# A feed-forward down projection with seven-product operands: the order of the products, the place of three kinds of stores and the pace of the operand fetches

## The chip, the cores and the metric

The kernel runs on one core of one Trainium2 chip. The time is that of the whole kernel on the device, in microseconds; of the kernel before, three runs are given. The core has a matrix engine (TensorE, PE in the profile), VectorE (DVE), ScalarE (ACT), GpSimd (POOL) and SyncE (SP), which here does nothing but issue DMAs, one after the other in the order of its queue.

## The reference

The reference is one layer of a hybrid transformer on 640 tokens (512 of a latent grid, 128 of a prompt): latent attention and a two-way RWKV-7 scan side by side, an output projection, and a SwiGLU feed-forward with post-normalisation. The change lies in the feed-forward, whose part is:

```python
def _swiglu(h, p):
    return (jax.nn.silu(h @ p["w_ffn_gate"]) * (h @ p["w_ffn_up"])) @ p["w_ffn_down"]
...
    x = _post_norm(x, g2, _swiglu(x * (1 + sc2) + sh2, p), p["ln2_g"], p["ln2_b"])
```

The model width is 2048, the hidden width 5632.

## The kernel before

**Seven products.** Gate, up and down projection are multiplied by a Strassen-like scheme. Two neighbouring 128-wide rows of the output and the two halves of the tokens (320 each) form a 2x2 block, and seven products of sums of blocks take the place of eight. Each product is written as three matmuls in a rounded format (high x high, high x low, low x high), 128x128 against 128x320.

**The right-hand operands.** For each pair of hidden tiles there are seven tiles of 128x640, numbered 0 to 6: tile 0 serves product 1, tiles 1 and 2 serve products 5 and 7, tiles 3 and 4 serve 4 and 6, tiles 5 and 6 serve 2 and 3. For the down projection they are made by `stored` (L1699), one step after each product of the next gate pair, with casts on ScalarE, differences on VectorE and subtractions on GpSimd, and go to DRAM (`hd`). There are 22 pairs of hidden tiles. The last pair has no gate pair behind it: its steps are kept as the generator `last` and run in the down projection's very first output pair (L1824).

**The weights.** `Quads.units` (L1372) loads four blocks 0 to 3 for each pair of output rows (`raw`, ten buffers, `N_R`), forms the seven sums in the order of the products, and splits each into high and low (`qh`, `ql`, four buffers, `N_Q`): a granule. A pair of the gate or up projection or of the down projection's pieces 1 to 3 has two granules for each product, one of piece 0 has one. Three granules are made ahead of the one that TensorE works on. Product 7 takes block 0 minus block 2 (GpSimd), product 5 the sum of 2 and 3, product 6 that less block 0 (both VectorE), product 4 block 3, product 2 block 1, product 3 block 1 less what stands in block 0 (GpSimd). Each block of the next pair is loaded where the same block of this pair is done with (`ahead`).

**The order of the products** is `ORDER` (L1329), for all three projections; `strassen` (L1437) walks through it, sends each product's result on with `out`, and calls `next(beside)` after each product.

**The down projection** runs over four pieces `c` of the hidden width, with 4, 6, 6 and 6 hidden pairs (`sizes`), and in each over eight pairs `j` of output rows. A piece needs 28 or 42 operand tiles in SBUF. The sums are carried in DRAM between the pieces: for each pair two `z` tiles are loaded (`sums_ahead`, L1804) and, a pair later, stored (`sums_behind`, L1811). Piece 3 makes products 1, 7, 5, 6, 3 of every pair first, and 2 and 4 at the end, beside the last normalisation.

**What sets the order.** SP's queue is in program order from the last up pair to the second pair of piece 3; everywhere else, and on the other engines, a scheduler with its own time line sets it. `Fetch` (L1722) fetches the operand tiles of the next piece: `step`, called at each granule, issues one as long as `room` allows; `room` is set at `j == 1` to `N_F - 7 * npr - 7` (28 in piece 0, 14 in pieces 1 and 2) and grows in the last pair as products let go of their tiles (`released`, L1750). What is missing when a product is written down is fetched there, by `operand` (L1743). SP waits, for each DMA, for the eighth DMA before it to land.

Of the kernel before, what the change touches and what calls it, by code (L numbers as in the profile page):

```python
# [157 lines left out]
def step_kernel(ctx: ExitStack, tc: tile.TileContext, a: dict, o: dict, upto: int = 99, npairs: int = NPAIR, dbg=None):  # L158
# [1169 lines left out]

    ORDER = (1, 7, 5, 6, 2, 3, 4)  # L1329

    class Quads:
# [40 lines left out]
        def units(self, pairs, begun=0, later=0):  # L1372
# [3 lines left out]
            for n, src in enumerate(pairs):  # L1376
                ng = src.shape[1]
                gs = range(ng)
                whole = n < len(pairs) - later
                q = nxt or {}  # L1380
# [6 lines left out]
                def ahead(k):  # L1387
                    if n + 1 < len(pairs):
                        for g in range(pairs[n + 1].shape[1]):
                            nxt[k, g] = self.load(pairs[n + 1][k, g])  # L1390
# [15 lines left out]
                ahead(2)  # L1406
                for g in gs:
                    if n >= begun and whole:
                        yield self.split(q[1, g])
                    tt(G, q[1, g], q[1, g], q.pop((0, g)), ALU.subtract)  # L1410
# [3 lines left out]
                ahead(1)  # L1414
                for g in gs if whole else ():
                    yield self.split(q.pop((3, g)))
                ahead(3)

# [303 lines left out]
    class Fetch:  # L1722
# [3 lines left out]
        def __init__(self, k0, n):  # L1726
            self.k0, self.t, self.room, self.count = k0, [[None] * 7 for _ in range(n)], 0, 0
            self.order = [(i, m) for q in ((0,), (1, 2), (3, 4), (5, 6)) for i in range(n) for m in q]

# [9 lines left out]
        def step(self):  # L1739
            if self.count < min(self.room, len(self.order)):  # L1740
                self.fetch()
# [8 lines left out]
        def released(self, n):  # L1750


            for m in ORDER:
                self.room += n * {1: 1, 5: 2, 3: 2, 4: 2}.get(m, 0)
                yield
# [15 lines left out]
    fetch = Fetch(0, 4)  # L1771
# [44 lines left out]
    def moved(c, j, n):  # L1816

        rel = fetch.released(n) if fetch and j == 7 else None
        for k in range(len(ORDER)):
            if k == 1:  # L1820
                sums_behind()
            if k == 2 and (c, j) != (3, 7):
                sums_ahead(*((c, j + 1) if j < 7 else (c + 1, 0)))
            if c + j == 0:  # L1824
                next(last, None)
            if rel:
                next(rel)
            yield

    sums_ahead(0, 0)  # L1830
    for c, (npr, ng) in enumerate(sizes):
        ops, k0 = fetch, k0 + npr
        fetch = qs.beside = Fetch(k0, sizes[c + 1][0]) if c < 3 else None
        for j in range(8):
            if j == 1 and fetch:
                fetch.room = N_F - 7 * npr - 7
# [170 lines left out]
```

## Time and profile before

| | us |
|---|---|
| median of 3 runs (lowest, highest) | 3575.87 (3572.85, 3577.72) |
| profiled execution: time, span | 3577.47, 3575.7 |
| TensorE busy in the span | 3391.9 (95%) |
| VectorE busy | 2627.2 (73%) |
| ScalarE busy | 1460.2 (41%) |
| GpSimd busy | 994.1 (28%) |
| first matmul of the down projection, from the span's start | 2916.33 |
| mean granted clock of TensorE | 0.959 |

All times in the views count from the start of the span. A row of a timeline shows when an instruction started, how long it took, its engine, line, operation and tiles, and in brackets how long the engine stood idle before it and what ended the wait. Buffer numbers are left out of the names: `op` is an operand tile, `hd` its place in DRAM, `raw` a block of weights, `b` a bank of PSUM, `z` a tile of sums and `zd` its place in DRAM, `p` and `t` the operand tiles that are made in SBUF.

### The profile page before, as it was taken

What the parts mean: (1) busy time and instruction counts of PE and PEld (TensorE: products, weight loads), DVE (VectorE), ACT (ScalarE), POOL (GpSimd) and SP (SyncE); (2) the same over time, 40 slices, a digit from 0 to 9 for tenths busy, and PEclk for the clock granted to TensorE, in tenths of its full rate; (3) what the DMA queues carried; (4) which work ended last, traced back from release to release, by engine and by line L of the source; (5) the groups of instructions that cost most, each with busy time, mean ns of one, the idle gap of its engine ahead of it and who ended that gap; (6) DMA issues with size and microseconds to landing.
All of it is one profiled execution on the core that took longest, in us unless ns stands there. A gap on an engine that the chain in (4) does not pass through costs nothing. (4 is left out here: it accounts for less than half of the span.)

```text
span 3575.7 us, 71303 instructions
## 1 busy us (share of the span) xinstructions
PE 3391.9 (95%) x27538; PEld 3032.9 (85%) x27538; DVE 2627.2 (73%) x4721; ACT 1460.2 (41%) x2987; POOL 994.1 (28%) x944
## 2 busy tenths in 40 slices
PE   8979999999999999999979999999999989999987
PEld 4667776777887778889979999999999989999987
DVE  1355676666676776667788988888888868778898
ACT  1143333333444444444453444444444434334334
POOL 0021111111111212111164544444444432222245
PEclk9988999999998999999989999999999999999997
DMA  8653444444112111066534443444433468666743
GB/s 296 236 171 125 142 152 138 155 153 137 60 58 86 37 41 37 18 215 196 154 113 136 165 129 128 133 138 138 136 124 127 143 227 296 234 245 213 257 126 106
DMA packets 289716, 529.05 MB, mean 148 GB/s; under 512 B 31008, under 2 KB 83680, under 8 KB 289376
## 3 DMA queue, kind: packets, MB, share of 16 engines
q1 hardware_dynamic: 289376, 524.49, 44.6%
q8 instruction: 216, 3.54, 0.4%
q14 instruction: 124, 1.02, 0.1%
HBM read 429.65 MB, written 93.09 MB: 146 GB/s over the span
## 5 line engine op out<-in xcount | busy, mean ns | idle before, releaser
L226 DVE TENSOR_TENSOR ql<-raw,qh 128x512 fp32r<-128x512 f32 (+1 forms) x1136 | 932.2, 834 | 282.9 <-ACT qh L1290 270.4
L1290 ACT CAST qh<-raw 128x512 fp32r<-128x512 f32 (+1 forms) x1136 | 661.0, 589 | 880.5 <-PE b L112 658.2
L226 POOL TENSOR_TENSOR raw<-raw,raw 128x512 f32<-128x512 f32 (+1 forms) x288 | 405.6, 1412 | 824.0 <-DVE ql L226 577.7
L112 PE MATMUL b<-t,qh 128*128 128x320 f32 x2816 | 626.9, 310 | 7.9 <-ACT qh L1290 6.8
L112 PE MATMUL b<-op,qh 128*128 128x320 f32 x2464 | 555.0, 318 | 26.0 <-DMA op<-hd 12.7
L112 PEld LDWEIGHTS b<-t,qh 128*128 128x128 f32 x2816 | 473.7, 189 | 9.1 <-ACT qh L1290 7.5
L112 PE MATMUL b<-p,qh 128*128 128x320 f32 x2112 | 468.2, 310 | 0.7 <-ACT qh L1290 0.7
L112 PEld LDWEIGHTS b<-op,qh 128*128 128x128 f32 x2464 | 422.2, 194 | 37.0 <-DMA op<-hd 15.7
L112 PE MATMUL b<-t,ql 128*128 128x320 f32 x1408 | 436.9, 311 | 5.8 <-DVE ql L226 5.8
L112 PE MATMUL b<-op,ql 128*128 128x320 f32 x1232 | 378.0, 319 | 17.0 <-DVE ql L226 17.0
L112 PEld LDWEIGHTS b<-p,qh 128*128 128x128 f32 x2112 | 354.3, 188 | 1.3 <-ACT qh L1290 1.2
L112 PE MATMUL b<-p,ql 128*128 128x320 f32 x1056 | 327.9, 311 | 7.0 <-DVE ql L226 7.0
L112 PEld LDWEIGHTS b<-t,ql 128*128 128x128 f32 x1408 | 265.2, 188 | 8.7 <-DVE ql L226 8.6
L112 PEld LDWEIGHTS b<-op,ql 128*128 128x128 f32 x1232 | 235.2, 194 | 25.4 <-DVE ql L226 25.0
L226 DVE TENSOR_TENSOR raw<-raw,raw 128x512 f32<-128x512 f32 (+1 forms) x288 | 246.4, 866 | 11.5 <-POOL raw L226 5.8
L112 PE MATMUL acc<-xh,whi 128*128 128x320 f32 x928 | 239.7, 341 | 0.3 <-DVE vS L1145 0.2
L112 PE MATMUL acc<-xh,wlo 128*128 128x320 f32 x928 | 235.6, 336 | 0.8 <-DVE wlo L226 0.8
L112 PE MATMUL b<-mh,qh 128*128 128x320 f32 x1024 | 229.6, 313 | 7.0 <-ACT qh L1290 7.0
L112 PE MATMUL acc<-xl,whi 128*128 128x320 f32 x928 | 236.2, 337 | 0.0
L112 PEld LDWEIGHTS b<-p,ql 128*128 128x128 f32 x1056 | 198.9, 188 | 9.4 <-DVE ql L226 9.4
L263 ACT CAST whi<-raw 128x512 fp32r<-128x512 f32 (+1 forms) x156 | 95.0, 609 | 257.1 <-PE acc L112 167.4
L226 DVE TENSOR_TENSOR wlo<-raw,whi 128x512 fp32r<-128x512 f32 (+1 forms) x156 | 107.3, 688 | 111.4 <-ACT whi L263 79.5
(328 smaller groups left out, 5847.5 us busy)
## 6 DMA issues: line engine op xcount, KB each, us to landing
wm<-in_w_mod_dram SPq DMA_DIRECT2D x64, 1024.0 KB, 5.4
op<-hd SPq DMA_DIRECT2D x154, 320.0 KB, 6.0
raw<-in_w_gate_dram SPq DMA_DIRECT2D x188, 256.0 KB, 2.7
raw<-in_w_up_dram SPq DMA_DIRECT2D x188, 256.0 KB, 2.8
raw<-in_w_down_dram SPq DMA_DIRECT2D x224, 192.0 KB, 3.5
raw<-in_w_in_dram SPq DMA_DIRECT2D x132, 256.0 KB, 2.7
wm<-in_w_mod_dram SPq DMA_DIRECT2D x64, 512.0 KB, 6.2
raw<-in_w_out_dram SPq DMA_DIRECT2D x128, 256.0 KB, 3.2
```

The costliest lines, as they stand in the source:

```text
L112: self.eng.matmul(out, lhsT, rhs, start=start, stop=stop)
L226: eng.tensor_tensor(out=out, in0=x, in1=y, op=op)
L263: A.copy(hi, r)
L1290: A.copy(hi, x)
```

## The change

The products come in the order 1, 7, 5, 6, 4, 2, 3, so block 3 of the weights is split ahead of block 1, and its successor is loaded ahead of those of blocks 0 and 1; the tiles 3 and 4 are let go ahead of 5 and 6. The stores of sums move from after the second product to after the fifth (`k == 4`), their loads from after the third to after the fourth (`k == 3`). The steps of `last` move from the first output pair of piece 0 to the third. `Fetch.step` issues at every second call until `released` starts, and in piece 0 the room for it opens at `j == 3` instead of `j == 1`.

```diff
@@ -1326,7 +1326,7 @@
                 out[t - 2] = third(*out[t - 2])
         return out
 
-    ORDER = (1, 7, 5, 6, 2, 3, 4)
+    ORDER = (1, 7, 5, 6, 4, 2, 3)
 
     class Quads:
 
@@ -1405,6 +1405,11 @@
                     yield self.split(q[0, g])
                 ahead(2)
                 for g in gs:
+                    if whole:
+                        yield self.split(q[3, g])
+                    del q[3, g]
+                ahead(3)
+                for g in gs:
                     if n >= begun and whole:
                         yield self.split(q[1, g])
                     tt(G, q[1, g], q[1, g], q.pop((0, g)), ALU.subtract)
@@ -1412,9 +1417,6 @@
                 for g in gs:
                     yield self.split(q.pop((1, g)))
                 ahead(1)
-                for g in gs if whole else ():
-                    yield self.split(q.pop((3, g)))
-                ahead(3)
 
     def product(qs, ops, ng, m):
         npr = len(ops) // ng
@@ -1725,6 +1727,7 @@
 
         def __init__(self, k0, n):
             self.k0, self.t, self.room, self.count = k0, [[None] * 7 for _ in range(n)], 0, 0
+            self.every, self.turn = 2, 0
             self.order = [(i, m) for q in ((0,), (1, 2), (3, 4), (5, 6)) for i in range(n) for m in q]
 
         def __len__(self):
@@ -1737,7 +1740,8 @@
             DMA.dma_start(out=t.bitcast(F32), in_=h_d[self.k0 + i][m])
 
         def step(self):
-            if self.count < min(self.room, len(self.order)):
+            self.turn += 1
+            if self.turn % self.every == 0 and self.count < min(self.room, len(self.order)):
                 self.fetch()
 
         def operand(self, i, m):
@@ -1750,8 +1754,9 @@
         def released(self, n):
 
 
+            self.every = 1
             for m in ORDER:
-                self.room += n * {1: 1, 5: 2, 3: 2, 4: 2}.get(m, 0)
+                self.room += n * {1: 1, 5: 2, 4: 2, 3: 2}.get(m, 0)
                 yield
 
     begun, beside = [], None
@@ -1817,11 +1822,11 @@
 
         rel = fetch.released(n) if fetch and j == 7 else None
         for k in range(len(ORDER)):
-            if k == 1:
+            if k == 4:
                 sums_behind()
-            if k == 2 and (c, j) != (3, 7):
+            if k == 3 and (c, j) != (3, 7):
                 sums_ahead(*((c, j + 1) if j < 7 else (c + 1, 0)))
-            if c + j == 0:
+            if c == 0 and j == 2:
                 next(last, None)
             if rel:
                 next(rel)
@@ -1832,7 +1837,7 @@
         ops, k0 = fetch, k0 + npr
         fetch = qs.beside = Fetch(k0, sizes[c + 1][0]) if c < 3 else None
         for j in range(8):
-            if j == 1 and fetch:
+            if fetch and j == (1 if c else 3):
                 fetch.room = N_F - 7 * npr - 7
             if j == 1 and c == 3:
                 loads.close()
```

On SP, at the entry into the down projection (`z` loads of the first pair, weights of the second pair, then the operand tiles 3 and 4 of piece 0 for product 6; `hd` written from `p` are the stores of the last SwiGLU pair), the queue before:

```order
L1589 DMA z_33008<-zd_17023 128x640
L1589 DMA z_33010<-zd_17024 128x640
L1708 DMA hd_17016<-p_5883_33034 128x640
L1354 DMA raw_33040<-in_w_down_dram 128x512
L1704 DMA hd_17021<-p_5888_33058 128x640
L1704 DMA hd_17022<-p_5889_33059 128x640
L1354 DMA raw_33067<-in_w_down_dram 128x512
L1589 DMA z_33085<-zd_17025 128x640
L1589 DMA z_33087<-zd_17026 128x640
L1354 DMA raw_33092<-in_w_down_dram 128x512
L1737 DMA op_33098<-hd_16872 128x640
L1737 DMA op_33100<-hd_16873 128x640
```

and of the change:

```order
L1591 DMA z_33008<-zd_17023 128x640
L1591 DMA z_33010<-zd_17024 128x640
L1354 DMA raw_33035<-in_w_down_dram 128x512
L1354 DMA raw_33054<-in_w_down_dram 128x512
L1354 DMA raw_33074<-in_w_down_dram 128x512
L1740 DMA op_33080<-hd_16872 128x640
L1740 DMA op_33082<-hd_16873 128x640
L1740 DMA op_33087<-hd_16879 128x640
L1740 DMA op_33089<-hd_16880 128x640
```

The three stores of the last SwiGLU pair are gone from this place, and the second pair's sums (`z_33085`, `z_33087` before) stand behind the eight fetches instead of ahead of them.

On SP, in the first pair of piece 1 (`op` fetched from `hd_16902` to `hd_16938` are the tiles of piece 1, `zd` written from `z` the last sums of piece 0), the queue before holds two fetches here and six more behind the last row:

```order
L1814 DMA zd_17053<-z_34153 128x640
L1814 DMA zd_17054<-z_34155 128x640
L1354 DMA raw_34509<-in_w_down_dram 128x384
L1354 DMA raw_34511<-in_w_down_dram 128x384
L1589 DMA z_34526<-zd_17041 128x640
L1589 DMA z_34528<-zd_17042 128x640
L1354 DMA raw_34546<-in_w_down_dram 128x384
L1354 DMA raw_34548<-in_w_down_dram 128x384
L1737 DMA op_34583<-hd_16916 128x640
L1737 DMA op_34585<-hd_16917 128x640
L1354 DMA raw_34590<-in_w_down_dram 128x384
L1354 DMA raw_34592<-in_w_down_dram 128x384
```

and of the change, from the weights of the second pair on:

```order
L1354 DMA raw_34481<-in_w_down_dram 128x384
L1354 DMA raw_34483<-in_w_down_dram 128x384
L1740 DMA op_34506<-hd_16908 128x640
L1740 DMA op_34511<-hd_16914 128x640
L1740 DMA op_34513<-hd_16915 128x640
L1354 DMA raw_34518<-in_w_down_dram 128x384
L1354 DMA raw_34520<-in_w_down_dram 128x384
L1740 DMA op_34526<-hd_16921 128x640
L1740 DMA op_34528<-hd_16922 128x640
L1740 DMA op_34533<-hd_16928 128x640
L1740 DMA op_34535<-hd_16929 128x640
L1740 DMA op_34540<-hd_16935 128x640
```

One more fetch of this group follows, then the loads and the stores of sums with two weight loads between them, and twelve fetches of tiles 5 and 6 in two groups of six: 21 in all, where there were eight.

On TensorE, in the first pair of piece 0, behind product 6 (bank `b_33091`; `b_33142` is product 2, `b_33181` product 3, `b_33210` product 4; `op_33149` is a tile 5), the rows before:

```order
L112 MATMUL b_33091<-op_33119,ql_33017 128x320
L112 MATMUL b_33142<-op_33149,qh_33042 128x320
L112 MATMUL b_33181<-op_33149,qh_33069 128x320
L112 MATMUL b_33210<-op_33098,qh_33094 128x320
L112 MATMUL b_33210<-op_33100,qh_33094 128x320
```

and of the change, behind product 6 (`b_33072`), with product 4 in `b_33123`:

```order
L112 MATMUL b_33072<-op_33101,ql_33017 128x320
L112 MATMUL b_33123<-op_33080,qh_33037 128x320
L112 MATMUL b_33123<-op_33082,qh_33037 128x320
L112 MATMUL b_33123<-op_33080,ql_33038 128x320
L112 MATMUL b_33123<-op_33087,qh_33037 128x320
```

Product 4, on tiles 3 and 4, is whole before the first matmul on a tile 5; before, one matmul each of products 2 and 3 stood ahead of it. In both, products 2 and 3 then alternate on the same tiles.

## The prediction

> **What bounds the kernel now.** I read the stages first. A row of the windows view gives, for a stretch, its length, TensorE's busy time with the matmuls, the same for its weight loads, VectorE, ScalarE and GpSimd, then granted clock, DMA share and GB/s.
>
> ```profile
> 2100.00:2150.00 50.00, 50.00 (x343) 50.00 (x342) 42.05 (x55) 22.07 (x39) 22.58 (x17) 1.00 0.41 133
> ```
>
> In the gate and up projections TensorE never idles and VectorE has 8 us in 50 to spare. Nothing is to be had there. Next the down projection, cut where its pieces and output pairs begin; rows of TensorE alone (length, busy time and matmuls, clock, DMA share, GB/s), counting only matmuls on fetched operand tiles (`op`). One that lies across an edge is counted in both rows.
>
> ```profile
> 2916.33:2945.95 29.62, 18.60 (x85) 0.71 0.84 315
> 2945.95:3039.15 93.20, 89.84 (x593) 1.00 0.79 286
> 3039.15:3062.64 23.49, 21.26 (x128) 0.93 0.89 318
> 3062.64:3102.02 39.38, 37.78 (x255) 1.00 0.69 240
> 3102.02:3120.50 18.48, 18.48 (x129) 1.00 0.48 157
> 3194.71:3221.49 26.78, 22.98 (x129) 0.87 1.00 365
> 3221.49:3260.31 38.82, 37.92 (x255) 1.00 0.71 251
> 3353.15:3375.35 22.20, 17.11 (x92) 0.85 0.98 354
> ```
>
> The fifth row is an undisturbed pair of piece 1: 126 matmuls (2 granules x 7 products x 9) in 18.48 us, so 0.1467 us each. At that rate a pair of piece 0 (84 matmuls) takes 12.3 us and one of piece 3 (90) 13.2. Against it the first pair of piece 0 loses 29.62 - 12.3 = **17.3 us**, its other seven 93.20 - 86.2 = **7.0**, the first pairs of pieces 1, 2 and 3 lose **5.0, 8.3 and 9.0**, and the two pairs after the first in pieces 1 and 2 lose 2.4 and 1.9. These 51 us are what the change can touch. Who is late, from TensorE's timeline and SP's (start, duration, operation, in brackets the idle time before it):
>
> ```profile
> 2921.47 0.31 PE L112 MATMUL b<-op,ql 128*128 128x320 f32 x1
> 2929.88 1.37 PE L112 MATMUL b<-op,qh 128*128 128x320 f32 x2 [8.10 <-ACT t L1290]
> 2938.63 1.40 PE L112 MATMUL b<-op,qh 128*128 128x320 f32 x4 [2.23 <-DMA op<-hd]
> ...
> 2901.87 0.98 SPq L1589 DMA_DIRECT2D z<-zd  x2
> 2913.65 0.32 SPq L1708 DMA_DIRECT2D hd<-p  x1
> 2914.07 0.38 SPq L1354 DMA_DIRECT2D raw<-in_w_down_dram  x1
> 2920.74 1.18 SPq L1704 DMA_DIRECT2D hd<-p  x2
> ...
> 2924.02 5.27 SPq L1737 DMA_DIRECT2D op<-hd  x8
> ```
>
> The wait of 8.10 us is put down to ScalarE, but the matmul reads an `op` tile, and the eight fetches for product 6 went out only at 2924.02. SP works in order: from 2902.9 to 2921.9 it stood behind three stores of the last SwiGLU pair. The waits view of SP names the first of them (total, times, longest), and, between 2960 and 3060, the stores of sums that hold it up in every later pair; the same view of ScalarE shows who is late there:
>
> ```profile
> SPq L1708 <- DVE p L226: 10.3, 1, 10.3
> ...
> SPq L1814 <- DVE z L235: 36.2, 9, 11.1
> ...
> ACT qh L1290 <- POOL raw L226: 17.8, 9, 3.1
> ```
>
> After the gap the clock is at half and the DMA engines are full:
>
> ```profile
> 2929.00:2943.00 14.00, 10.21 (x28) 0.50 1.04 403
> ```
>
> **Term 1, first pair of piece 0.** The change takes those stores out of this pair. Ahead of the eight fetches now stand the sums' loads and three weight loads. The last of the three needs a buffer that GpSimd's second subtraction of the last up pair frees. Before, that was the end of this row, three operations in a row:
>
> ```profile
> 2902.03 4.26 POOL L226 TENSOR_TENSOR raw<-raw,raw 128x512 f32<-128x512 f32 x3 [12.78 <-DMA op<-hd]
> ```
>
> Now product 4's two granules stand ahead of it, 2 x 12 x 0.1467 = 3.5 us, so about 2909.8: the fetches start 14 us earlier. At 403 GB/s a tile of 328 KB takes 0.81 us, eight take 6.5; with some 2.5 us of latency the last lands near 2919, and product 6 starts at 2916.33 + 3 x 1.76 = 2921.6. Behind them come two loads of sums (1.6 us), a weight load (0.65) and the eight tiles for products 2 and 3 (6.5): served from 2918.8 to 2925.3, landed by 2922.9 to 2927.8. Product 4 now stands ahead of 2 and 3, so these are needed from 2925.1 to 2927.7. I leave 0.8 us: **-16.5**. Bounds: -17.3 with no wait; -9, if a wait like that of piece 2 (8.3) remains.
>
> **Term 2, the other pairs of piece 0.** Before, pairs 1 to 4 fetched one tile of piece 1 at every granule: per pair 4 x 262 KB of weights, 7 tiles, 2 sums in and 2 out, 4.7 MB, where 12.3 us at 403 GB/s carry 5.0, and SP stood 36.2 us in 100 behind stores of sums. Weights then came late to GpSimd's subtraction, and ScalarE waited for it (17.8). With fetches at every second granule from pair 3 on, a pair moves 3.5 MB. The stores stand three products further back in the queue, behind all weight loads for the next pair; SP may wait at them as before, but by then those loads are out: **-6**, bounds -7 and 0.
>
> The postponed stores (7 transfers of 0.81 us, three casts, three differences, the subtractions) fall into pair 2, which has no fetch: 1.0 + 1.3 + 2.3 = 4.7 MB, as before in pairs 1 to 4, but over queues that are ahead. I cost them at 0; without that cover at about 1 us, the loss of such a pair.
>
> **Term 3, into piece 1: the price.** Piece 1 needs 42 tiles. Before, 28 came during pairs 1 to 4 and 6 in pair 7, so 34 were there and 8 fetched on demand. Now pairs 3 to 6 bring 14 and pair 7 brings 7: 21, and **21 on demand**. Those go out between weight loads whose buffers free themselves as TensorE moves on. The row of before nearest to it is the start of piece 2, with 16 on demand:
>
> ```profile
> 3200.90 6.63 SPq L1737 DMA_DIRECT2D op<-hd  x10
> ...
> 3206.37 0.42 PE L112 MATMUL b<-op,qh 128*128 128x320 f32 x1 [2.41 <-DMA op<-hd]
> ```
>
> There the queue reached the fetches 6.2 us into the piece, and the first was usable 5.5 us later. Now no store's wait stands ahead, and I let the first three go out at 2.3 us and the rest flow from 4: 18 tiles, 2 sums in, 2 out (22 x 0.81) and 6 weight loads of 197 KB (0.49) make 20.8 us; with 2.5 of latency and the last six matmuls at half clock (1.6) the pair ends at 29 to 29.5 instead of 23.49: **+6**. Bounds: +3 (flow from 1.8 us), +13 (flow from 6.2, at 318 GB/s as in the third row of the table).
>
> **Term 4, into pieces 2 and 3.** As many tiles on demand as before (16). In piece 2 the 12 tiles for products 2 and 3 now stand behind two loads and two stores of sums (4 x 0.81 = 3.2 us), but are needed one product (2.64 us) later: **+1**. Piece 3 has no products 2 and 4 here, so nothing is needed later, and two loads (1.6 us) stand in between; the wait for a store ahead of all goes: **+1**. Bounds for each: -3 and +3.
>
> **Term 5, what follows.** After a long wait the pairs behind it may start at a low clock: **+1**. After the long gap three matmuls took 0.80 us, 0.267 each:
>
> ```profile
> 2940.10 0.73 PE L112 MATMUL b<-op,qh 128*128 128x320 f32 x2
> 2940.63 0.47 PE L112 MATMUL b<-op,ql 128*128 128x320 f32 x1
> 2940.90 0.73 PE L112 MATMUL b<-op,qh 128*128 128x320 f32 x2
> ```
>
> Bounds: 0, and +4.4 for two products at that rate (18 x 0.12 = 2.2 each). In the gate and up projections products 2, 3 and 4 only trade places under a TensorE that is always fed: 0. The later pairs of piece 3 and the end keep their instructions, in another order here and there: 0, bounds -2 and +2 for both together.
>
> Sum: -16.5 - 6 + 6 + 1 + 1 + 1 = **-13.5 us**. The profiled execution took 3577.47 us (span 3575.7), so 3564.0; it lies 1.6 above the median shown, 3575.87, from which I predict 3562.4, **3563**.
>
> Two rules of the Trainium skill bear on terms 3 and 5. Its page "DMA: Bandwidth & Descriptors", in "Where 436 GB/s comes from", says that for traffic to and from HBM the limit of a core is about 358 GB/s; by that, the 22 big transfers of term 3 would take an estimated 0.92 us each, 2.4 us more in all, and the sum would be -11. The row of 403 GB/s over 14 us speaks against it. Its page "TensorE: Matmul & The Clock Gate", in "What's actually happening", has the full rate back after one busy window of about 3.4 us; by that term 5 would be 0 and the sum -14.5. The row of 14 us at 0.50, though with a further wait of 2.2 us in it, does not bear that out.
>
> **The rivals.**
> (a) *The gain is given back at the seams.* Fetches on demand are paced by buffers that TensorE frees, and TensorE waits for the fetches. Term 3 at its upper bound and term 4 at its: -13.5 + 7 + 2 + 2 = -2.5, 3573. For it: the DMA share of 1.00 over the first pair of piece 2. Against it: the queue loses its waits for stores.
> (b) *It doesn't do what it says.* The eight fetches stay late because the third weight load waits for GpSimd past 2918; a gap like piece 2's remains, term 1 is -9: -13.5 + 7.5 = -6, 3570. Against it: GpSimd was done at 2906.3.
> (c) *Slower: the first weights of a pair are late.* In the new order of loads, the tile of product 1 of the next pair is asked for two granules ahead of its split, where it was four. Its buffer comes free with the split of granule 9, which starts when TensorE is through granule 5 (four buffers of split weights); it is needed for granule 14. That is eight granules of 1.32 us, 10.6 us in piece 1, less two splits of 1.4 (589 and 834 ns by the first rows below). If a load takes longer than the 7.8 us left, every pair waits. If each of the 14 later pairs of pieces 1 and 2 lost 1.6 us, that is +22: 3585, and the gate and up pairs would add to it. Against it: these loads land in 3.5 us at the median.
>
> ```profile
> L226 DVE TENSOR_TENSOR ql<-raw,qh 128x512 fp32r<-128x512 f32 (+1 forms) x1136 | 932.2, 834 | 282.9 <-ACT qh L1290 270.4
> L1290 ACT CAST qh<-raw 128x512 fp32r<-128x512 f32 (+1 forms) x1136 | 661.0, 589 | 880.5 <-PE b L112 658.2
> ...
> raw<-in_w_down_dram SPq DMA_DIRECT2D x224, 192.0 KB, 3.5
> ```
>
> **How the numbers follow.** Forecast 0.73, (a) 0.14, (b) 0.05, (c) 0.08. About 0.2% (7.2 us) is what a measurement of this kernel can tell from no change. The forecast lies beyond it, (a) and (b) within, (c) beyond on the other side: 0.73, 0.19, 0.08. The range starts at 3554: term 3 at +3, term 4 at -1 each and term 5 at 0 come to 3554.4. It ends at 3575, past (a) and (b); outside remain (c) and some tenth of the rest.
>
> **What would show it.** Term 1: no wait of TensorE above 1 us between 2916 and 2930, the eight fetches out before 2916, and a first pair of about 13 us. Term 2: pairs of 12.3 to 12.6 us in piece 0, and no wait of ScalarE for GpSimd that reaches TensorE there. Term 3: a first pair of piece 1 near 29 us, with a gap before product 2. Term 4: first pairs of 26 to 30 and 21 to 25 us. The forecast is wrong if piece 1 opens with more than 36 us, or if TensorE gets gaps inside the gate and up projections.

## The result, and the profile after

The changed kernel takes **3555.39 us** (median of 5 runs, 3546.88 to 3558.5) where the kernel before, run five times too, takes 3574.07 (3571.19 to 3577.72). The ratio is 0.994, with a 95% interval of 0.9923 to 0.9956. The profiled execution is the one of 3555.39 us, with a span of 3553.6, 22.1 shorter than the span of before. By the medians the kernel is 18.7 us shorter. The forecast was 13.5 shorter: right in its sign, too small in its size.

The stretches below are cut as in the prediction, about where the matmuls on fetched tiles of a pair begin (an exact count of the matmuls puts the edges up to ten of them, 1.8 us, earlier; the tables go by that count): the first pair of piece 0, its other seven, the first pair of piece 1, the two behind it, the same for piece 2, and the first pair of piece 3 (windows view, TensorE's matmuls on `op` tiles alone: length, busy time and matmuls, clock, DMA share, GB/s).

```profile
2912.05:2925.62 13.57, 12.99 (x85) 1.00 1.04 398
2925.62:3012.76 87.14, 87.14 (x591) 1.00 0.83 293
3012.76:3044.10 31.34, 24.05 (x129) 0.84 0.87 319
3044.10:3081.21 37.11, 37.11 (x256) 1.00 0.81 275
3174.04:3201.08 27.04, 22.46 (x131) 0.87 0.93 334
3201.08:3238.33 37.25, 37.25 (x256) 1.00 0.81 274
3330.88:3355.28 24.40, 17.98 (x92) 0.79 0.90 313
```

The first pair is down from 29.6 to 13.6 us, and the seven behind it (second row) run without any idle time: 87.14 busy in 87.14. The first pair of piece 1 has become longer, 31.3 instead of 23.5. What no term of the forecast has is in rows four and six: the second and third pairs of pieces 1 and 2 run without a gap too, where before they lost 2.4 and 1.9 us.

One part of the 22.1 us lies ahead of everything that the change touches. The view of the tiles `p` says when the gate and up projections begin (first start after the comma). It is one row each of before, of the changed kernel, and of a second profile of the changed kernel, taken in the run after_again below:

```profile
L112 PE MATMUL b<-p,qh x2112: 302/309/634, 1792.5 to 2912.5; 128*128 128x320 f32 x192
```

```profile
L112 PE MATMUL b<-p,qh x2112: 302/309/468, 1788.4 to 2911.8; 128*128 128x320 f32 x192
```

```profile
L112 PE MATMUL b<-p,qh x2112: 302/309/633, 1795.1 to 2918.4; 128*128 128x320 f32 x192
```

The changed kernel reached that point 4.1 us earlier in one execution and 2.6 us later in the other. So spans are compared from there on: 3575.7 - 1792.5 = 1783.2 us before, 1765.2 and 1763.2 after. **The change itself is worth 18 to 20 us in these profiles.** The length of a pair in the tables is the time that its number of matmuls on fetched tiles takes (84, 126 or 90), counted off in the trace. In TensorE's queue a pair's first matmuls stand among the last ones of the pair before it, so a wait near a seam can fall to either of the two, and sums over neighbouring pairs say more than one pair.

| stretch, us | before | changed | again | change measured | forecast |
|---|---|---|---|---|---|
| gate and up projections | 1123.8 | 1123.6 | 1123.6 | -0.2, -0.2 | 0 |
| first pair of piece 0 (term 1) | 29.6 | 13.4 | 13.1 | -16.2, -16.5 | -16.5 |
| pairs 1 to 7 of piece 0 (term 2) | 92.9 | 87.1 | 86.4 | -5.8, -6.5 | -6 |
| first pair of piece 1 (term 3) | 23.5 | 31.3 | 30.6 | +7.8, +7.1 | +6 |
| first pairs of pieces 2 and 3 (term 4) | 49.0 | 50.9 | 50.9 | +1.9, +1.9 | +2 |
| pairs 1 to 7 of pieces 1 and 2 (term 5) | 262.8 | 258.7 | 258.7 | -4.1, -4.1 | +1 |
| piece 3 from its second pair on, and the end | 201.5 | 200.1 | 199.9 | -1.4, -1.6 | 0 |

### The profile page after: what moved, and what is told of

It is laid out like the page before. It is cut to its first block, busy times and chain, and to the rows that moved or that the text cites. A ratio compares the mean times of both kernels' runs of the same rounds, so it can differ in the third digit from the quotient of the medians.

```text
span 3553.6 us, 71134 instructions
## 1 busy us (share of the span) xinstructions
PE 3376.3 (95%) x27538; PEld 3022.9 (85%) x27538; DVE 2609.0 (73%) x4721; ACT 1459.1 (41%) x2987; POOL 992.5 (28%) x944
## 3 DMA queue, kind: packets, MB, share of 16 engines
q14 instruction: 123, 1.01, 0.1%
## 4 chain that ended last, share of the span: by engine, by line
PE 55%; DVE 6%; issue 2%; DMA 2%; ACT 1%; POOL 1%; SPq 0%; ACTq 0%; DVEq 0%; POOLq 0%
PE b L112 47%; PE acc L112 3%; PE m L112 3%; DVE ql L226 1%; DMA op<-hd 1%; PE x L112 1%; DVE z L226 1%; POOL z L226 1%; PE acc L116 0%; DMA raw<-in_w_down_dram 0%; DVE z L235 0%; DVE ns L226 0%; DVE raw L226 0%; ACT nd L565 0%; DVE u L226 0%
## 5 line engine op out<-in xcount | busy, mean ns | idle before, releaser
L226 POOL TENSOR_TENSOR raw<-raw,raw 128x512 f32<-128x512 f32 (+1 forms) x288 | 397.0, 1380 | 852.2 <-DVE ql L226 654.4
L112 PE MATMUL b<-op,qh 128*128 128x320 f32 x2464 | 547.0, 315 | 18.3 <-DMA op<-hd 18.0
L112 PE MATMUL b<-op,ql 128*128 128x320 f32 x1232 | 375.2, 317 | 19.7 <-DVE ql L226 19.5
L226 DVE TENSOR_TENSOR raw<-raw,raw 128x512 f32<-128x512 f32 (+1 forms) x288 | 216.5, 764 | 12.5 <-POOL raw L226 10.6
```

The lines of the kernel that those rows point to most:

```text
L112: self.eng.matmul(out, lhsT, rhs, start=start, stop=stop)
L226: eng.tensor_tensor(out=out, in0=x, in1=y, op=op)
```

## The experiments

Thirteen runs, of eleven kernels: after_again is the changed kernel and c1_again is c1_every1 once more. First the edits one by one on the kernel of before (e), then taken out of the changed kernel (f), then numbers changed (c, d) and the order of the weight loads taken apart (g). The column "to the end" is the profiled span less the start of the gate and up projections; the others are pair lengths in us, (piece, pair), in the last two columns those of the second and the third pair of a piece. A ratio is to the kernel before, with its 95% interval.

| kernel | ratio | to the end | (0,0) | (0,1-7) | (1,0) | (1,1), (1,2) | (2,1), (2,2) |
|---|---|---|---|---|---|---|---|
| before | 1 | 1783.2 | 29.6 | 92.9 | 23.5 | 19.5, 19.8 | 18.8, 19.8 |
| changed | 0.9940 (0.9923 to 0.9956) | 1765.2 | 13.4 | 87.1 | 31.3 | 18.5, 18.5 | 18.5, 18.5 |
| after_again | 0.9947 (0.9929 to 0.9965) | 1763.2 | 13.1 | 86.4 | 30.6 | 18.5, 18.5 | 18.5, 18.5 |
| e1_last | 0.9978 (0.9967 to 0.9989) | 1769.5 | 12.3 | 99.2 | 21.9 | 19.0, 20.0 | 18.8, 19.9 |
| e2_sums | 0.9999 (0.9987 to 1.0012) | 1778.3 | 29.8 | 89.5 | 21.6 | 19.9, 18.5 | 19.9, 18.5 |
| e3_fetch | 1.0020 (1.0007 to 1.0033) | 1787.0 | 28.5 | 92.7 | 32.7 | 18.5, 18.5 | 19.0, 19.5 |
| e4_order | 1.0061 (1.0039 to 1.0083) | 1795.6 | 25.1 | 97.1 | 22.4 | 22.8, 20.4 | 21.2, 20.8 |
| f2_sums_back | 1.0027 (1.0016 to 1.0038) | 1789.5 | 12.3 | 101.4 | 30.6 | 20.4, 19.4 | 19.8, 22.0 |
| f4_order_back | 0.9982 (0.9971 to 0.9993) | 1773.9 | 13.4 | 90.8 | 31.9 | 19.9, 18.5 | 19.9, 18.5 |
| c1_every1 | 0.9931 (0.9913 to 0.9949) | 1750.5 | 12.8 | 86.4 | 21.1 | 18.5, 18.6 | 18.5, 18.5 |
| c1_again | 0.9923 (0.9906 to 0.9939) | 1754.3 | 13.7 | 86.3 | 21.7 | 18.5, 18.5 | 18.5, 18.5 |
| c2_room1 | 0.9952 (0.9934 to 0.9970) | 1764.9 | 12.3 | 94.3 | 25.6 | 18.5, 18.5 | 18.5, 18.5 |
| g1_third_last | 0.9966 (0.9954 to 0.9978) | 1769.8 | 13.8 | 91.6 | 29.8 | 18.5, 18.5 | 18.5, 18.5 |
| g2_first_last | 0.9941 (0.9924 to 0.9957) | 1762.6 | 12.6 | 90.2 | 30.1 | 18.5, 18.5 | 18.5, 18.5 |
| d1_two | 0.9904 (0.9887 to 0.9921) | 1746.6 | 12.3 | 91.6 | 19.2 | 18.5, 18.8 | 18.5, 20.2 |

The expectations give the lengths of single pairs by a rougher count, up to 1 us off these.

### One edit at a time, on the kernel of before

**e1_last**, the stores alone:

```diff
-            if c + j == 0:
+            if c == 0 and j == 2:
                 next(last, None)
```

> The kernel of before with one edit: the stores of the last SwiGLU pair are issued in pair 2 of piece 0 instead of pair 0. Theory A (each edit has its own place): only the first pair of piece 0 changes, from 29.6 us to 14-15 us (13.6 in the changed kernel, where product 4 also stands ahead of 2 and 3), pairs 1 to 7 of piece 0 stay at 93 us together or grow by up to 3, because the stores now lie beside the fetches of pairs 1 to 4; the whole 13 to 16 us shorter, ratio 0.9955 to 0.9965. Rival B (the first pair needs the new order of products): products 2 and 3 still wait for their operands, the pair stays above 18 us, the whole under 12 us shorter.

The first pair falls to 12.3 us, the ideal, so moving the late stores is enough to cure it; rival B falls. But the stores are not free where they now stand. The windows view of e1_last, first pair and third pair of piece 0:

```profile
2921.83:2934.15 12.32, 12.32 (x85) 1.00 1.04 399
2948.40:2966.46 18.06, 14.72 (x86) 0.91 1.02 391
```

The third pair takes 18.1 us at full DMA engines, and pairs 1 to 7 together 6.3 more than before, above the 3 of theory A. The whole is 0.22% shorter (about 8 us by the ratio, 13.7 in the profile), less than theory A's 0.9955 to 0.9965.

**e2_sums**, the place of the sums alone:

```diff
-            if k == 1:
+            if k == 4:
                 sums_behind()
-            if k == 2 and (c, j) != (3, 7):
+            if k == 3 and (c, j) != (3, 7):
```

> The kernel of before with one edit: the sums of the pair behind are stored at product 5 instead of 2 (counting from 1) and the next sums loaded at product 4 instead of 3. Theory A (weight loads stood in SP's queue behind stores that wait): pairs 1 to 7 of piece 0 fall from 93.2 us to about 89 (half or more of the 6.1 that the whole change brought), the second and third pairs of pieces 1 and 2 from 20.2, 19.2, 19.7 and 19.2 to 18.5-18.7 each, which is the 4 us that the forecast had not counted; the whole 6 to 10 us shorter. Rival B (those gains come from the sparser fetches and what they leave of the DMA engines): nothing moves in either place, the whole within 2 us.

Half missed. Pairs 1 to 7 of piece 0 gain 3.4 of the 5.8 us, but the second pairs stand at 19.9, and the whole is unchanged by the ratio (0.9999; 4.9 us shorter in the profile). The third pairs are cured (18.5 in both pieces).

**e3_fetch**, the sparser fetches alone:

```diff
+            self.turn += 1
-            if self.count < min(self.room, len(self.order)):
+            if self.turn % self.every == 0 and self.count < min(self.room, len(self.order)):
...
-            if j == 1 and fetch:
+            if fetch and j == (1 if c else 3):
```

> The kernel of before with one edit: operands of the next piece are fetched at every second granule, and in piece 0 from pair 3 on instead of pair 1. Theory A: the first pair of piece 1 grows by 8 us (23.5 to about 31), pairs 1 to 7 of piece 0 lose at most 2 of their 93.2 us, because the stores of sums still hold the weight loads; first pairs of pieces 2 and 3 within 1 us; the whole 5 to 8 us longer. Rival B: pairs 1 to 7 of piece 0 fall by 5 to 6 us as the fetches make room, the whole within 3 us of before.

As theory A has it: +9.2 us in the first pair of piece 1, only -0.2 in the pairs before it, 0.2% slower. What it had not: the second and third pairs of piece 1 fall to 18.5 behind the longer first one, while those of piece 2 stay at 19.0 and 19.5.

**e4_order**, the order of products and weights alone:

```diff
-    ORDER = (1, 7, 5, 6, 2, 3, 4)
+    ORDER = (1, 7, 5, 6, 4, 2, 3)
...
                 ahead(2)
+                for g in gs:
+                    if whole:
+                        yield self.split(q[3, g])
+                    del q[3, g]
+                ahead(3)
...
                 ahead(1)
-                for g in gs if whole else ():
-                    yield self.split(q.pop((3, g)))
-                ahead(3)
```

> The kernel of before with one edit: the product order 1 7 5 6 4 2 3 and the weights' order that goes with it. Theory A: no pair moves by more than 1 us but the first of piece 0 (product 4's operands are there, products 2 and 3 are needed 3.5 us later: up to 2 us either way) and the first of piece 3 (nothing is needed later there); gate and up stay 1123.9 us; the whole within 3 us. Rival B (the third and fourth weights of a pair asked for earlier are what cured the second and third pairs of pieces 1 and 2): these fall from 20.2, 19.2, 19.7 and 19.2 to 18.5-18.7, 4 us in all.

Both theories fall: **alone the new order is 0.61% slower**, about 22 us. Pairs 1 to 7 of piece 0 lose 4.2, the second and third pairs together 3.8 in piece 1 and 3.4 in piece 2. In the second pair of piece 1 (3058.86 to 3082.28) the timeline of e4_order has one gap of TensorE, at its very end, ahead of the third pair's first matmul. The waits view of ScalarE says that it waits for weights there, that of SP names the store of sums (total, times, longest):

```profile
3081.32 0.83 PE L112 MATMUL b<-op,qh 128*128 128x320 f32 x2 [4.11 <-ACT qh L1290]
```

```profile
ACT qh L1290 <- DMA raw<-in_w_down_dram: 8.4, 1, 8.4
...
SPq L1816 <- DVE z L235: 9.1, 1, 9.1
```

SP stands 9.1 us before a store whose sum isn't there yet, and the new order has more weight loads behind it: the next pair's tile for product 1 is asked for two granules later. This is the mechanism of rival (c) of the prediction, set off by the store.

Added up, the four edits alone give -13.7 - 4.9 + 3.8 + 12.4 = -2.4 us in the profiles, and by the ratios (-0.22, -0.01, +0.20 and +0.61%) a loss of 0.58%, about 21 us; together they give -18 to -20. They don't add.

### One edit taken out of the changed kernel

**f2_sums_back** puts the sums back (k == 1 and k == 2):

> The changed kernel with one edit undone: sums stored at product 2 and loaded at product 3 again (counting from 1). Theory C (the edits work together: the new order of weights makes every wait of a sums store worse, as the kernel of before with the new order alone showed, 12.4 us longer from the gate and up projections to the end, and only with the stores behind the weight loads is it harmless): the second pairs of pieces 1 and 2 rise from 18.5 to 22-23 us, pairs 1 to 7 of piece 0 from 87.1 to 93 or more; the whole 12 to 18 us longer than the changed kernel, ratio to before 0.997 to 1.000. Rival D (the order alone was slow because of the stores of the last SwiGLU pair and the fetches at every granule): second pairs stay below 19.5 us, pairs 1 to 7 of piece 0 below 90, the whole within 5 us of the changed kernel.

Theory C, and in the whole by more than it said: 24 us longer than the changed kernel, and slower than before (the second pairs, at 20.4 and 19.8, lose less than its 22 to 23). With the new order, the stores of sums *must* stand behind the weight loads. The waits view of SP over pairs 1 to 7 of piece 0, f2_sums_back (102 us), the changed kernel (87 us) and the kernel before (93 us):

```profile
SPq L1819 <- DVE z L235: 53.5, 7, 11.7
```

```profile
SPq L1819 <- DVE z L235: 31.9, 6, 7.3
```

```profile
SPq L1814 <- DVE z L235: 40.0, 9, 11.1
```

SP waits for the sums in the changed kernel as well, 32 us in 87; before it was 40 in 93. Most of that wait is still there. What changed is what stands behind it: TensorE has no wait at all there.

**f4_order_back** puts the order of products and weights back:

> The changed kernel with one edit undone: product order 1 7 5 6 2 3 4 and the old order of weights. Theory C: the three other edits without the order bring about what they brought one by one (-13.7, -4.9 and +3.8 us from the gate and up projections to the end, less what the late stores cost in pairs 1 to 5 of piece 0, since these have fewer fetches beside them): 1764 to 1770 us where before has 1783.2 and the change 1765.2; second pairs of pieces 1 and 2 stay at 19.7-20. Rival E (the order is what cured the second pairs and what the postponed stores need): second pairs 19.7-20 and, besides, pairs 1 to 7 of piece 0 above 92 us: 1772 us or more.

1773.9 us, 9 to 11 longer than the changed kernel: rival E's range. The second pairs are back at 19.9, as both theories had it (the third ones stay at 18.5), and pairs 1 to 7 of piece 0 are at 90.8, a little short of its 92. In the second pair of piece 1 it is another wait than in e4_order. TensorE's timeline and ScalarE's waits of f4_order_back:

```profile
3066.20 0.55 PE L112 MATMUL b<-op,qh 128*128 128x320 f32 x2 [0.96 <-ACT qh L1290]
```

```profile
ACT qh L1290 <- DVE raw L226: 3.9, 4, 1.5
```

ScalarE waits for VectorE's sum of the blocks 2 and 3 of the weights, for product 5, early in the pair. e2_sums has the same two figures (0.96 and 3.9). So each edit alone leaves or makes a wait that the other one takes away.

### Which part of the order it is

**g1_third_last** asks for the third tile (block 3 of the weights, the third to be loaded) last again, with the new order of products:

```diff
                     del q[3, g]
-                ahead(3)
...
                 ahead(1)
+                ahead(3)
```

> The changed kernel with one line moved: the third weight tile of the next pair is asked for last again, as before; the order of products, the place of the sums and all else as in the changed kernel. Theory C (with the stores out of the way, the second pairs of pieces 1 and 2 lost their time waiting for that tile, which product 5 needs through VectorE's sum): second pairs rise from 18.5 to about 20, with the loss in their second product slot, as in the two kernels that have late stores and the old order; pairs of piece 0 to 12.5-13.5; the whole 4 to 9 us longer than the changed kernel. Rival G (it is the order of the products themselves): second pairs stay at 18.5-18.7, the whole within 3 us.

The second pairs stay at 18.5, so being asked for last is not by itself what hurts: theory C falls there, though the whole is 4.6 and 6.6 us longer than the two profiles of the changed kernel, as it had it. Piece 0 does lose (91.6, with 16.5 in the pair that has the postponed stores), and the ratio is 0.9966 beside 0.9947 for the changed kernel on the same chip, with intervals that overlap. **g2_first_last** goes the other way: f4_order_back, with the old order of products, and the third tile asked for one place earlier, the second last:

```diff
-                ahead(1)
+                ahead(3)
                 for g in gs if whole else ():
                     yield self.split(q.pop((3, g)))
-                ahead(3)
+                ahead(1)
```

> The changed kernel with the old order of products, as in the kernel with the order undone, and one swap on top: of the next pair's weights the third is asked for where the second was, and the second last, behind the pair's last split. Theory I (the late one is the tile whose buffer only the last split frees; in the old order this was the third, which product 5 needs early in the next pair, in the new order it is the second, needed for product 2): second pairs of pieces 1 and 2 fall from 20.1 to 18.5-18.7 us with the old order of products too, pairs 1 to 7 of piece 0 from 91 to 87-90; the whole 3 to 8 us shorter than with the order undone. Rival G (the order of the products decides, wherever the tiles are asked for): second pairs stay at 20.0-20.1, the whole within 2 us of it.

Swapping two loads brings the second pairs to 18.5, and the whole from 0.9982 to 0.9941, the ratio of the changed kernel and more than the 3 to 8 us of theory I. The windows view of the second pair of piece 1, f4_order_back and g2_first_last:

```profile
3059.65:3079.73 20.08, 19.12 (x130) 1.00 0.75 242
```

```profile
3042.26:3060.89 18.63, 18.63 (x129) 1.00 0.83 273
```

The timelines say how. SP's of f4_order_back has the third tile (the second row) behind the stores of sums, then VectorE's first sum that needs it; the same two engines of g2_first_last have the third tile in the first row, ahead of the stores:

```profile
3054.37 0.82 SPq L1817 DMA_DIRECT2D zd<-z  x2
3055.75 1.18 SPq L1354 DMA_DIRECT2D raw<-in_w_down_dram  x2
...
3062.78 0.55 DVE L226 TENSOR_TENSOR raw<-raw,raw 128x384 f32<-128x384 f32 x1
```

```profile
3029.49 1.16 SPq L1354 DMA_DIRECT2D raw<-in_w_down_dram  x2
...
3035.75 1.78 SPq L1817 DMA_DIRECT2D zd<-z  x2
...
3038.21 1.36 DVE L226 TENSOR_TENSOR raw<-raw,raw 128x384 f32<-128x384 f32 x1 [0.91 <-POOL raw L226]
```

In f4_order_back the tile goes out 3.9 us ahead of its pair (3059.65), and VectorE's first sum of it comes 3.1 us into the pair; in g2_first_last it is 12.8 us ahead, and the sum is begun 4.1 us before the pair (3042.26). In f4_order_back the two loads took 5.9 us to land (median; DMA view, 3053 to 3060), so to about 3061.7 and 3062.5, and the sum at 3062.78 follows them closely:

```profile
raw<-in_w_down_dram SPq DMA_DIRECT2D x2, 192.0 KB, 5.9
```

In g1_third_last the tile is asked for last and yet goes out 8.5 us ahead (at 3045.53, behind two loads of block 1, for the pair at 3054.01). So **the order of the products was not needed in pieces 1 and 2**: what the new order brought there is the third tile in time. That its buffer is the reason, as theory I had it, these runs don't show; SP's waits of f4_order_back from 3045 to 3057 speak against it, with 0.3 us at weight loads for VectorE's splits:

```profile
SPq L1354 <- DVE ql L226: 0.3, 1, 0.3
```

What stood ahead of the tile there was six fetches and the two stores (from 3048.18 on). In piece 0 theory I missed: 90.2 us, where 87 to 90 were expected. What is left there (1.9 us above the undisturbed 12.3 in the pair with the stores, up to 0.9 in the others) goes with the order of products or with that of the other loads, in which the two kernels differ; which of them does it was not tried.

### The fetches

**c1_every1** and **c1_again** are the changed kernel with one number:

```diff
-            self.every, self.turn = 2, 0
+            self.every, self.turn = 1, 0
```

> The changed kernel with one number changed: fetches at every granule instead of every second (in piece 0 still from pair 3 on). Theory C (what the fetches cost was the wait behind stores of sums, which is gone): 35 instead of 21 tiles of piece 1 are there at its start, its first pair falls from 31.3 to 22-24 us, pairs 3 to 6 of piece 0 rise by under 1 us each; the whole 4 to 8 us shorter than the changed kernel. Rival D (a pair with 7 tiles has more traffic than the DMA engines carry): pairs 3 to 6 at 13.3-14 us as before, which gives 4 to 7 us back: no gain.

> The changed kernel with fetches at every granule, once more, beside the changed kernel on the same chip. Theory C: 10 to 15 us shorter than the changed kernel (first pair of piece 1 21 instead of 31 us, first pair of piece 3 2 us shorter), 1750 us within 3 from the gate and up projections to the end, ratio to before 0.990 to 0.993. Rival: the two are within 4 us, and what the first pair of piece 1 gains is lost in piece 3.

Both times the first pair of piece 1 is back at 21 to 22 us and pairs 1 to 7 of piece 0 stay at 86.4 and 86.3: theory C, though the second time its bounds for the whole are missed by about 1 us (1754.3, and 8.9 shorter than after_again). From the gate and up projections to the end it is 9 to 15 us shorter than the changed kernel; by the medians on one chip 3547.76 against 3555.3, with intervals of the two ratios that overlap a little. So, by the pair lengths, **the sparser pace is a loss**: it costs 9 to 10 us at the start of piece 1 and gives nothing back. For the time of the whole the evidence is weaker, as the overlap says.

**c2_room1** keeps every second granule and starts with 14 tiles at pair 1:

```diff
-            if fetch and j == (1 if c else 3):
-                fetch.room = N_F - 7 * npr - 7
+            if fetch and j in ((1,) if c else (1, 3)):
+                fetch.room = 14 if c == 0 and j == 1 else N_F - 7 * npr - 7
```

> The changed kernel with one edit: in piece 0 14 tiles may already be fetched from pair 1 on, still at every second granule, so that 28 instead of 21 tiles of piece 1 are there at its start. Theory C: the first pair of piece 1 falls from 31.3 to about 27 us (the first pair of piece 2, with the same 14 to 16 tiles on demand, takes 27.0), pairs 1 and 2 rise by under 1 us each; the whole 3 to 4 us shorter than the changed kernel. Rival D: pair 2, where the postponed stores lie, rises from 12.8 to 15 us or more and takes it back.

The first pair of piece 1 comes to 25.6, but the pairs ahead of it rise from 87.1 to 94.3 (14.0, 15.7, 14.6 and 13.1 for pairs 1 to 4): rival D, no gain. Behind the postponed stores, at twice the density (c1), fetches are free. That it is the fetches beside the stores that are dear is not shown: in d1_two below, pairs 1 and 2 are nearly as long with hardly a fetch beside them.

**d1_two** is c1_every1, and fetches two tiles a granule while a last pair frees them:

```diff
-            self.every, self.turn = 2, 0
+            self.every, self.turn, self.burst = 1, 0, 1
...
-            if self.turn % self.every == 0 and self.count < min(self.room, len(self.order)):
-                self.fetch()
+            for _ in range(self.burst):
+                if self.count < min(self.room, len(self.order)):
+                    self.fetch()
...
-            self.every = 1
+            self.burst = 2
```

> The kernel with fetches at every granule, and two at every granule in the last pair of a piece (and of the up projection), where the old operands come free. Theory C (the first pairs of pieces 2 and 3 wait because 18 tiles are still to be issued when they begin): up to 12 tiles more are there, the first pair of piece 2 falls from 26.4 to 20-23 us and that of piece 3 from 22.3 to 17-20. Rival H (the DMA engines are what is short there: two pairs around the seam move 15 MB where 37 us at 403 GB/s carry 14.9, or SP stands before tiles that are not yet free): the last pairs of pieces 1 and 2 lose what the first pairs gain, the whole within 3 us or longer.

The lowest ratio of all: 0.9904 (0.9887 to 0.9921), median 3538.68 us of four runs. The windows view of d1_two, the first pairs of pieces 1, 2 and 3:

```profile
3024.38:3043.58 19.20, 18.76 (x129) 1.00 0.97 340
3173.85:3194.71 20.86, 19.16 (x130) 1.00 1.01 366
3326.24:3345.32 19.08, 15.85 (x92) 0.86 1.01 363
```

20.9 and 19.1 us in pieces 2 and 3 are as theory C has it, and the last pairs of pieces 1 and 2 lose nothing (18.5 each). The DMA engines are full there (0.97 to 1.01), yet TensorE is busy for 98, 92 and 83% of these pairs: what the first pairs lacked was tiles asked for in time, more than engines to carry them. Pairs 1 and 2 of piece 0 rise to 14.0 and 15.3 us, though SP's first fetch for piece 1 goes out at 2955.52, late in pair 2, and the third pair of piece 2 to 20.2; why was not looked into, and it is still to be had.

### The same kernel again

**after_again**:

> The changed kernel once more, unedited. Theory C (what precedes the gate and up projections differs from execution to execution and has nothing to do with the change): that part takes anything from 1787 to 1800 us, while the rest repeats: 1765 us from the gate and up projections to the end within 3, each pair of pieces 0 to 2 within 0.5 us. Rival F: the 4.1 us that the first part of the changed kernel was shorter come back, 1788.4 within 1 us, and are part of the change.

Theory C: the start moved by 6.7 us, the rest repeated within 2.0; the largest difference of a pair in pieces 0 to 2 is 0.7, in the first of piece 1, a little over its 0.5.

## Why the forecast was right or wrong, step by step

**Term 1, right**, -16.5 against -16.2 and -16.5. The eight fetches for product 6 went out 14 us earlier, as worked out: 7.7 us behind the first pair's start before, 6.4 ahead of it (2912.05) now. SP's timeline of the changed kernel:

```profile
2905.68 5.14 SPq L1740 DMA_DIRECT2D op<-hd  x8
...
2913.19 5.91 SPq L1740 DMA_DIRECT2D op<-hd  x8
```

One argument of it was not needed: product 4 ahead of 2 and 3. With the old order the pair is even shorter (12.3, e1_last).

**Term 2, right in size (-6 against -5.8 and -6.5), half right in its reason.** The stores behind the weight loads do it, but only with the new place of the weights (f4_order_back 90.8, f2_sums_back 101.4). Of the other reason that it gave, fewer fetches, the sparser pace is worth nothing (c1, 86.4 and 86.3); the later start may be worth something (c2, 94.3). The postponed stores at no cost: right for the changed kernel (12.8 us in that pair), and that it was the queues' being ahead that covered them is argued, not shown; put into the kernel before (e1_last), they cost 4.6 us there, where the prediction had about 1 without that cover.

**Term 3, a little small, and not by its mechanism**: +6 against +7.8 and +7.1. The rest of the tiles did not flow. SP's timeline of the changed kernel in the first pair of piece 1, which begins at 3012.76, then TensorE's:

```profile
3017.75 1.34 SPq L1740 DMA_DIRECT2D op<-hd  x3
...
3020.09 3.65 SPq L1740 DMA_DIRECT2D op<-hd  x6
...
3029.12 4.51 SPq L1740 DMA_DIRECT2D op<-hd  x6
...
3035.59 5.50 SPq L1740 DMA_DIRECT2D op<-hd  x8
```

```profile
3025.79 0.56 PE L112 MATMUL b<-op,qh 128*128 128x320 f32 x2 [1.54 <-DMA op<-hd]
...
3035.66 1.38 PE L112 MATMUL b<-op,qh 128*128 128x320 f32 x3 [4.88 <-DMA op<-hd]
```

They went in four batches, 5.0, 7.3, 16.4 and 22.8 us into the piece, where the forecast let them flow from 4. The last two of the 23 are tiles of piece 2, so 21 were issued on demand, as forecast. The waits view of SP over this pair has weight loads among what stood between the batches, waiting for VectorE's splits:

```profile
SPq L1354 <- DVE ql L226: 10.1, 5, 5.7
```

**Term 4, right** within its bounds: 0.0 and +1.9 (again: +0.3 and +1.6), forecast +1 and +1. That they add up to nearly the forecast 2 is partly luck.

**Term 5 is the step that failed.** It said that the pairs behind a long wait may start at a low clock, +1, with 0 as its best case; measured is -4.1 and -4.1. First, the clock was back before the pair ended. The windows view of the changed kernel behind the gap of 4.88 us (here with all of TensorE's matmuls):

```profile
3036.00:3038.00 2.00, 2.00 (x8) 0.50 1.04 393
3038.00:3040.00 2.00, 2.00 (x9) 0.50 1.06 392
3040.00:3042.00 2.00, 1.80 (x10) 0.96 1.03 393
3042.00:3044.00 2.00, 2.00 (x16) 1.00 1.04 396
```

About 4.5 us of work at half rate, then the full one; the pair at 3044.10 starts at 1.00. The 14 us that the forecast went by held 3.8 us of idle time: behind the last gap in them, which ends at 2938.63, the timeline of before has matmuls 0.27 us apart until 2942.8 and 0.15 from 2943.01 on, 4.4 us later. The page "TensorE: Matmul & The Clock Gate" of the Trainium skill, in "What's actually happening", gives about 3.4 us for this, which is nearer to these rows than 14 us. Second, and this is the larger part, the 2.4 and 1.9 us of the second and third pairs were listed among what the change can touch, and then no term took them up. The reason of term 2 holds in pieces 1 and 2 too: the stores' place alone cures the third pairs (e2), and e4, f2, f4 and g2 show that these pairs lose their time to loads that stand behind other work in the same queue.

**The end.** 0 within 2 was forecast for piece 3 behind its first pair and all that follows; it was -1.4 and -1.6. Pairs of that piece differ by up to 1.3 us between two profiles of one kernel (the last one 16.0 in c1_every1, 17.3 in c1_again), and whether the change moved any of them was not tried.

**Gate and up projections**, 0: right (-0.2). Of the 22.1 us between the two profiles, 4.1 lie ahead of them, where both kernels have the same instructions; no forecast could have had them.

Against the forecast, then, terms 1 to 4 together were 2.2 us too low in the first profile and 0.5 in the second, term 5 was 5.1 too high in both, the end 1.4 and 1.6, the gate and up projections 0.2: that makes the -18.0 and -19.9 of -13.5.

**The rivals.** (a), the gain given back at the seams, took place in part (+9.7 and +9.0 us at the three first pairs), far from its bound. (b) did not happen. (c), slower because the first weights of a pair come late, did not happen either, but it was the right fear: e4_order and f2_sums_back lose time in the second, the third and the last pairs of pieces 1 and 2, and where e4_order was looked at, in the second pair of piece 1, it is set off by a store that waits, not by the load's 3.5 us.

## What to carry to other kernels

In a queue that works in order, don't ask only what waits, ask what stands behind it: in pairs 1 to 7 of piece 0 SP still waited 32 us behind stores of sums after the change, of 40 before, and TensorE had no wait there, with the weight loads ahead of the stores. Edits of one queue need not add: alone these gained 2 us in the profiles and lost time by the ratios, together they gained 18 to 20, and one that helps in company (the order) costs 0.6% by itself, so test by taking out as well as by putting in. And when a term's reason is found in one stage, go through the list of losses and ask in which other stages it holds.

## What the runs showed that was not expected

The same instructions do not take the same time in each execution, ahead of the change as well: the gate and up projections began between 1784.4 us (c1_again) and 1799.6 (f4_order_back). The granted clock differs with it; from 300 to 500 us, c1_again and f4_order_back:

```profile
300.00:500.00 200.00, 188.06 (x2283) 0.97 0.46 149
```

```profile
300.00:500.00 200.00, 188.58 (x2221) 0.93 0.45 144
```

Short waits were enough here to halve the clock. Behind waits of 0.39, 1.54 and 0.27 us, which end at 3023.4, 3025.8 and 3026.6 in the changed kernel, matmuls on the timeline begin 0.27 us apart until 3029.8, and 0.15 from 3030.2 on; the granted clock was 0.50 from 3027 to 3029.

The DMA engines carried 398 GB/s through the first pair of the changed kernel, at a share of 1.04, beside a TensorE that idled for 0.6 us in 13.6. The page "DMA: Bandwidth & Descriptors" of the Trainium skill, in "Where 436 GB/s comes from", puts the limit to and from HBM at about 358 GB/s; here, as in the prediction's row, the trace shows more.
